# Attention preparation in small steps: 1/rms through ScalarE's ln and exp, and q and k scaled by ScalarE one token tile at a time

## The chip, the cores and the metric

The kernel runs on one core of a Trainium2 chip. The metric is device time in microseconds for one execution of the whole program (two layers of the trunk), median over runs. Five engines matter: TensorE (PE in the profile, with its weight loads as PEld), VectorE (DVE), ScalarE (ACT), GpSimd (POOL) and SyncE (SP), which issues the DMAs.

## The reference, cut to what matters

Two request groups share all weights: 128 context tokens ("prompt") and 1024 latent tokens. The change touches only the latent attention of each layer:

```
c_kv = _rmsnorm(kv_lat, kv_norm_g)
q = (_rmsnorm(q_lat, q_norm_g) @ w_q_up).reshape(b, t, MLA_HEADS, QK_HEAD)      # 8 heads of 96
q = _rmsnorm(q, q_head_g)
k, v = _mla_kv(c_kv, k_pe, w_kv_up, k_head_g)      # k = rmsnorm([k_nope 64, k_pe 32]) per head
if latent:
    q = jnp.concatenate([q[..., :64], _rope_2d(q[..., 64:])], axis=-1)
    k = jnp.concatenate([k[..., :64], _rope_2d(k[..., 64:])], axis=-1)
    k, v = concatenate with the cached context's k_c, v_c      # 1152 keys
attn = softmax(q k^T * 96 ** -0.5) v      # context tokens attend to themselves alone
```

So each token needs, per head, 1/rms of its 96 q elements and of its 96 k elements, a rotation of 32 of them, and a multiplication of all 96 by that 1/rms.

## The kernel before, in words

The eight heads are worked in four pairs. Everything is float32; a product that must be exact is split into a high and a low part and done as three matmuls.

`pair_prep` (L931) prepares a pair. For each of ten token tiles of 128 tokens (0 is the prompt, 1 to 8 the latent tokens, 9 the cached context) it issues nine matmuls (L960 to L969) into one PSUM tile, copies q, k and v out on ScalarE (L971 to L974) and collects sums of squares into `ssq` (L979, L981), then yields. After the ten tiles come a chain on VectorE: the sums are completed (L984 to L988), 1/rms is taken by `rsq` (L231: an integer guess and three Newton rounds, eleven instructions of 40 elements a partition), and for each half b of the tokens q is rotated (`rope`, L918 to L921), q is multiplied by 1/rms (L995, 768 elements a partition) and so is k (L997 for the 64 plain elements of each head, L998 for the rotated 32).

`prompt` (L1009) does the whole attention of the 128 context tokens of the pair: scaling (L1016 to L1019), transposes (L1022), scores (L1029), softmax (L1031 to L1039), and output (L1043 to L1050).

`head_prep` (L1057) transposes k and q of one head (L1070), splits them (L1073, L1074), then computes for 8 query tiles by 3 key chunks a score block (L1081) and its row maximum on VectorE (L1083), takes the maximum over all keys (L1087), negates it (L1088), transposes it (L1090) and writes it into the query operand (L1092).

`head_main` (L1098) is the attention of one head over nine key tiles. For each key tile: two halves of three score matmuls (L1127 to L1129) and an exp on ScalarE each (L1130) into PSUM tiles of which there are three; then, after a yield, the products with v (L1110) and, on GpSimd, the running sum of the exponentials (L1113, L1119, L1117). `head_end` (L1146) divides by that sum; it is issued in the next head's first key tile: L1153 on PE, L1157 and L1158 on ScalarE, L1159, L1160 and L1162 on VectorE.

The order of the work comes from `attention` (L1168). While `head_main` of head h runs, two side generators are advanced at each of its 18 or 19 yields: `heads()` (the next heads' `head_prep`, up to a weight RA per yield) and `pairs()` (the next pair's `pair_prep`, then GAP empty steps, then `prompt`, then the loads for the next stage), RB steps per yield. A pair's heads may start only when `R["ready", p]` is set. The framework then shifts neighbouring instructions a little. Each engine runs its own queue strictly in order, so one matmul that waits for VectorE holds everything behind it on PE.

Pair 0 and head 0 are prepared in the same way under the input projection (`in_proj`), in steps called from L783.

Of the kernel before, what the change touches and what calls it, by code (L numbers as in the profile page):

```python
# [25 lines left out]
P = 128  # L26
# [21 lines left out]


CT, CM, CB, RX = 0.7, 1.4, 0.7, 0.5  # L50
RA, RB, LEAD, GAP = 1.3, 0.7, 14, 5


def segs(c):
# [22 lines left out]
class Net:  # L77
# [653 lines left out]
    def in_proj(self, l, h, R, ticks):  # L731
        nc, a = self.nc, self.a
        rk, rv = R["rk"], R["rv"]
        rq, rg = [], []
        mix = R["mix"] = [None] * 8
        bg = []

        def step(n):
            for _ in range(n):
                while bg and next(bg[0], bg) is bg:  # L740
                    bg.pop(0)
        yc = {}
        for i in range(2, len(IN_FM)):
            name = IN_FM[i]
            kind, j = name[:2], int(name[2]) if name[2:] else int(name[1]) if name[1:].isdigit() else 0
            w = self.get(("in", l, i))
            if kind in ("rq", "rg", "gc"):
                dst = self.S(name)
            if kind == "q0":
                R["qn"] = [[self.S("qh", dt=F32R) for _ in range(2)], [self.S("ql", dt=F32R) for _ in range(2)]]  # L750
                sqq = self.S("sqq")
                qg = self.v("q_norm", l)
                pc = self.ax((P, 9, 1))
            if kind == "kv":
                R["ckv"] = [self.S("ch", dt=F32R), self.S("cl", dt=F32R)]
                kg = self.v("kv_norm", l)
                pc = self.ax((P, 9, 1))
                R["ckvo"] = self.sm("ckvo", (P, P), bufs=1)
            for c in range(3):
                cs = slice(c * CH, (c + 1) * CH)  # L760
                ps = self.mm()
                self.fm(w, h, KD, c, ps)
                if kind == "rg":
                    silu = nc.scalar.activation(dst[:, cs], ps, AF.Silu)
                elif kind == "xi":
                    self.conv_u(gc, u, ps, c)
                elif kind == "gb":
                    nc.vector.tensor_tensor(yc[j][:, cs], yc[j][:, cs], ps, op=ALU.mult)
                elif kind in ("q0", "q1"):
                    self.gain_split(ps, qg[:, j:j + 1], R["qn"][0][j][:, cs], R["qn"][1][j][:, cs])  # L770
                    if j == 0:
                        nc.scalar.activation(sqq[:, cs], ps, AF.Square)
                    else:
                        self.lat_sum(ps, pc, c == 0, c == 2, 3 * c, sqq[:, cs])
                elif kind == "kv":
                    self.gain_split(ps, kg, R["ckv"][0][:, cs], R["ckv"][1][:, cs])
                    self.lat_sum(ps, pc, c == 0, c == 2, 3 * c)
                    if c == 0:
                        nc.scalar.activation(R["ckvo"], ps[:, 0:P], AF.Copy, scale=kg)
                else:  # L780
                    nc.scalar.copy(dst[:, cs], ps)
                self.tick(ticks)
                step(3)  # L783
            if kind == "rq":
                rq.append(dst)
            elif kind == "gc":
                gc = dst
                u = gc
            elif kind == "xi":
                yc[j] = self.S("yc")  # L790
                self.conv_y(l, j, u, yc[j])
            elif kind == "gb":
                mix[j] = self.spill(yc[j])
            elif kind == "rg":
                rg.append(dst)
            elif kind == "q1":

                R["qms"] = self.sm("qms", (P, 9), bufs=1)
                nc.vector.tensor_scalar(R["qms"], pc.rearrange("p a b -> p (a b)"), EPS / 256, EPS * EPS, ALU.mult, ALU.add)
            elif kind == "kv":  # L800
                self.kv_scale(l, R, pc)
            if name == "rq1":
                bg.append(self.retention(l, rq, rk, rv, rg, mix))
            if name == "kv":
                step(1000)

                with self.tc.issue_after(silu.ins):
                    nc.scalar.preload_act_table_set("natural_log_exp_and_others")
            if name == "kv":
                self.mla_tables(l, R)  # L810
                self.pair_weights(l, 0, R)
                bg += [self.pair_prep(l, 0, R), self.head_prep(l, 0, R), self.prompt(l, 0, R)]
        step(1000)
# [98 lines left out]
    def rope(self, x, tab, out=None):  # L912
# [7 lines left out]
        nc.vector.tensor_tensor(out[:, :, :, 0:16], t1[:, :, :, 0:16], t2[:, :, :, 16:32], op=ALU.subtract)  # L920
        nc.vector.tensor_tensor(out[:, :, :, 16:32], t2[:, :, :, 0:16], t1[:, :, :, 16:32], op=ALU.add)  # L921

    def pair_weights(self, l, p, R):
        if ("w", p) not in R:
            raw = self.W()[:, :640]
            self.nc.sync.dma_start(out=raw, in_=self.a["w_qkv"][l, p])
            R["w", p] = self.S("qwh", (P, 640), F32R), self.S("qwl", (P, 640), F32R)
            self.hilo(raw, *R["w", p])
        return R["w", p]

    def pair_prep(self, l, p, R):  # L931
# [22 lines left out]
        for t in range(10):  # L954
# [25 lines left out]
            for j in range(2):  # L980
                nc.scalar.activation(sq[:, j, 0:64], kvp[:, j * 64:(j + 1) * 64], AF.Square, accum_out=ssq[:, 2 + j, t:t + 1])  # L981
            yield
        V = nc.vector
        V.tensor_tensor(ssq[:, 2:4, :], ssq[:, 2:4, :], R["kvs2"].unsqueeze(1).to_broadcast([P, 2, 10]), op=ALU.mult)  # L984
        V.tensor_tensor(ssq[:, 2:4, :], ssq[:, 2:4, :], R["kpss"].unsqueeze(1).to_broadcast([P, 2, 10]), op=ALU.add)
        V.tensor_scalar(ssq[:, 2:4, :], ssq[:, 2:4, :], 1.0 / 96, EPS, ALU.mult, ALU.add)
        V.scalar_tensor_tensor(ssq[:, 0:2, 0:9], ssq[:, 0:2, 0:9], 1.0 / 96,
                               R["qms"].unsqueeze(1).to_broadcast([P, 2, 9]), ALU.mult, ALU.add)  # L988
        r = self.rsq(ssq, (P, 4, 10))
        yield  # L990
        for b in range(2):
            self.rope(q[b][:, :, :, 64:96], R["rtab"][:, :, 4 * b:4 * b + 4])
            t0, n = 1 + 4 * b, 4 + b
            bc = lambda i, n, m: r[:, i:i + 2, t0:t0 + n].rearrange("p a b -> p b a").unsqueeze(3).to_broadcast([P, n, 2, m])
            V.tensor_tensor(q[b], q[b], bc(0, 4, 96), op=ALU.mult)  # L995
            yield
            V.tensor_tensor(k[b][:, :, :, 0:64], k[b][:, :, :, 0:64], bc(2, n, 64), op=ALU.mult)  # L997
            V.tensor_tensor(k[b][:, :, :, 64:96],  # L998
                            R["kper"][:, t0:t0 + n, :].unsqueeze(2).to_broadcast([P, n, 2, 32]), bc(2, n, 32), op=ALU.mult)
            yield  # L1000
        R["tm", p] = (lambda t: q[t // 4][:, t % 4], lambda t: k[min(t // 4, 1)][:, t - 4 * min(t // 4, 1)], vv)
        R["pr", p] = pr, prv, r
# [6 lines left out]
    def prompt(self, l, p, R):  # L1009
# [3 lines left out]
        at = self.attn_tile(p, R)  # L1013
        gains = self.gains(l)
        for hh in range(2):
            V.tensor_tensor(pr[:, hh, 64:96], pr[:, hh, 64:96], R["gq"], op=ALU.mult)  # L1016
            V.tensor_scalar(pr[:, hh, :], pr[:, hh, :], r[:, hh, 0:1], None, ALU.mult)
            V.tensor_scalar(pr[:, 2 + hh, 0:64], pr[:, 2 + hh, 0:64], r[:, 2 + hh, 0:1], None, ALU.mult)
            V.tensor_scalar(pr[:, 2 + hh, 64:96], R["kper"][:, 0, :], r[:, 2 + hh, 0:1], None, ALU.mult)  # L1019
        pt = self.ax((96, 4, P))  # L1020
        for i in range(4):
            nc.tensor.transpose(pt[:, i, :], pr[:, i, :], self.ident)  # L1022
# [6 lines left out]
            nc.tensor.matmul(ps[:, hh, :], qk[:, hh, :], qk[:, 2 + hh, :], start=True, stop=True)  # L1029
        m, den = self.sm("pm", (P, 2)), self.sm("pden", (P, 2))  # L1030
        V.reduce_max(m, ps, axis=AX.X)  # L1031
        V.tensor_scalar(m, m, -SCALE, None, ALU.mult)
        pp = self.Tt("pp", (P, 2, P))
        for hh in range(2):
            nc.scalar.activation(pp[:, hh, :], ps[:, hh, :], AF.Exp, scale=SCALE, bias=m[:, hh:hh + 1],
                                 accum_out=den[:, hh:hh + 1])
        V.reciprocal(den, den)
        for hh in range(2):
            V.tensor_scalar(pp[:, hh, :], pp[:, hh, :], den[:, hh:hh + 1], None, ALU.mult)  # L1039
        yield  # L1040
        pt = self.ax((P, 2, P))
        for hh in range(2):
# [14 lines left out]
    def head_prep(self, l, h, R):  # L1057
# [20 lines left out]
        for qt in range(8):  # L1078
            for c in range(3):
                ps = self.ax((P, CH))  # L1080
                nc.tensor.matmul(ps, qh[0:96, qt * P:(qt + 1) * P], kh[0:96, c * CH:(c + 1) * CH],  # L1081
                                 start=True, stop=True)
                nc.vector.reduce_max(mx[:, qt, c:c + 1], ps, axis=AX.X)  # L1083
                yield CM / 3
        yield CB
        mn = self.sm("mn", (P, 8))
        nc.vector.reduce_max(mn, mx, axis=AX.X)  # L1087
        nc.vector.tensor_scalar(mn, mn, -1.0, None, ALU.mult)  # L1088
        pt = self.ax((8, P))
        nc.tensor.transpose(pt, mn, self.ident)  # L1090
        o, _ = VEC["eye8"]
# [76 lines left out]
    def attention(self, l, R, x):  # L1168
# [10 lines left out]
        def pairs():  # L1179
            for p in range(1, 4):  # L1180
                yield from self.pair_prep(l, p, R)
                if p < 3:
                    self.pair_weights(l, p + 1, R)
                for _ in range(GAP):
                    yield
                R["ready", p] = True
                yield
                yield from self.prompt(l, p, R)
            while self.head_lim < 7:
                yield  # L1190
# [571 lines left out]
```

## Time and profile before

| | |
|---|---|
| median of 3 runs | 3169.8 us (3165.72 to 3171.39) |
| the profiled execution: its own time, its span | 3169.16 us, 3167.4 us |
| busy in the span: PE / DVE / ACT / POOL | 96% / 56% / 35% / 37% |
| attention of layer 0, of layer 1 (us of the span) | about 340 to 700, 1905 to 2260 |

A share of busy time is a mean over all stages; the two attention stretches are the ones this change touches, and they are read by themselves below. PEclk is the clock granted to TensorE as a share of 2.4 GHz: 0.50 is 1.2 GHz, and a value between the two is a mean over a window with both.

### The profile page before, as it was taken

The numbers are of one execution on the slowest core, as the hardware profiler recorded it, in microseconds if no ns is written. First come the engines' busy times: TensorE is split into PE (matmuls) and PEld (weight loads), VectorE is DVE, ScalarE is ACT, GpSimd is POOL, SyncE is SP. The second block draws the span as 40 slices with busy tenths as digits, with TensorE's granted clock in tenths as the row PEclk, the third lists the DMA queues.
The fourth block names the chain that finished last, engine by engine and source line by source line (L and its number), as shares of the span: only waits on it lengthen the run. The fifth ranks groups of instructions, "written<-read, shape, count | busy, mean of one in ns | idle before, by whom it ended". The sixth has DMA issues, their size and how long they took to land.

```text
span 3167.4 us, 48782 instructions
## 1 busy us (share of the span) xinstructions
PE 3033.0 (96%) x19136; PEld 2686.3 (85%) x19136; DVE 1778.7 (56%) x3483; ACT 1113.2 (35%) x2646; POOL 1178.4 (37%) x764
## 2 busy tenths in 40 slices
PE   6999999999799999999999999899988999999999
PEld 5988855459799999998999896554788999999999
DVE  6264476766954555633272646767588455556343
ACT  4333455444522222321153235454444222223211
POOL 3111243465643443411242103434656434343212
PEclk8999998999899999999999999999998999999999
DMA  5323000123222122576231110010322222226323
GB/s 211 103 95 128 22 12 1 60 91 107 83 81 74 63 84 81 178 251 237 66 113 48 49 32 13 12 53 8 121 100 69 84 84 71 69 71 220 101 67 100
DMA packets 126726, 278.06 MB, mean 88 GB/s; under 512 B 24097, under 2 KB 47393, under 8 KB 126497
## 3 DMA queue, kind: packets, MB, share of 16 engines
q1 hardware_dynamic: 126496, 274.95, 25.8%
q8 instruction: 151, 2.47, 0.3%
q14 instruction: 79, 0.64, 0.1%
HBM read 222.57 MB, written 52.33 MB: 87 GB/s over the span
## 4 chain that ended last, share of the span: by engine, by line
PE 81%; DVE 12%; DMA 2%; ACT 2%; issue 2%; POOL 1%; SPq 0%; DVEq 0%; POOLq 0%; ACTq 0%
PE mm L227 14%; PE mm L229 14%; PE mm L228 14%; PE ax L227 6%; PE ax L229 6%; PE ax L228 6%; PE ax L1110 5%; PE ax L1081 2%; PE mm L1127 2%; PE mm L1129 2%; PE mm L1128 1%; PE ax L325 1%; PE ax L1070 1%; DVE mx L1083 1%; POOL W L213 1%
## 5 line engine op out<-in xcount | busy, mean ns | idle before, releaser
L213 POOL TENSOR_TENSOR W<-r,W 128x512 fp32r<-128x512 f32 x336 | 447.8, 1346 | 541.7 <-ACT W L212 530.7
L213 POOL TENSOR_TENSOR W<-W,W 128x640 fp32r<-128x640 f32 (+5 forms) x168 | 298.4, 1777 | 827.9 <-ACT W L212 477.1
L227 PE MATMUL mm<-gh,W 128*128 128x384 f32 x1056 | 354.8, 336 | 1.9 <-DVE u L1401 1.1
L229 PE MATMUL mm<-gh,W 128*128 128x384 f32 x1056 | 353.3, 335 | 0.9 <-POOL W L213 0.8
L228 PE MATMUL mm<-gl,W 128*128 128x384 f32 x1056 | 352.9, 334 | 0.0
L1246 DVE SCALAR_TENSOR_TENSOR x<-mm,mod,x 128x128 f32<-128x128 f32 (+2 forms) x320 | 157.9, 515 | 329.7 <-PE mm L229 327.6
L229 PE MATMUL ax<-hth,W 128*128 128x288 f32 x1056 | 314.6, 298 | 10.1 <-POOL W L213 10.1
L227 PE MATMUL ax<-hth,W 128*128 128x288 f32 x1056 | 314.8, 298 | 7.6 <-ACT W L212 7.6
L228 PE MATMUL ax<-htl,W 128*128 128x288 f32 x1056 | 314.1, 298 | 0.0
L1119 POOL TENSOR_TENSOR W<-W,W 128x1024 f32<-128x1024 f32 x96 | 230.8, 2404 | 222.2 <-ACT W L1130 220.6
L212 ACT CAST W<-r 128x512 fp32r<-128x512 f32 x336 | 205.2, 621 | 184.8 <-DMA r<-in_w_up 63.8
L212 ACT CAST W<-W 128x640 fp32r<-128x640 f32 (+5 forms) x168 | 131.5, 783 | 390.6 <-DMA W<-in_w_down 178.7
L1083 DVE TENSOR_REDUCE mx<-ax 128x1 f32<-128x384 f32 x384 | 195.7, 550 | 115.2 <-PE ax L1081 112.8
L1130 ACT ACTIVATE W<-mm 128x512 f32<-128x512 f32 x288 | 168.5, 605 | 218.1 <-PE mm L1129 210.6
L227 PE MATMUL mm<-hh,W 128*128 128x384 f32 x704 | 240.5, 342 | 0.0
L229 PE MATMUL mm<-hh,W 128*128 128x384 f32 x704 | 239.0, 339 | 0.0
L228 PE MATMUL mm<-hl,W 128*128 128x384 f32 x704 | 237.9, 338 | 0.0
L1110 PE MATMUL ax<-W,vt 128*64 128x512 f32 x576 | 208.4, 658 | 8.2 <-DVE attn L1162 6.7
L229 PEld LDWEIGHTS ax<-hth,W 128*128 128x128 f32 x1056 | 201.2, 191 | 11.3 <-POOL W L213 11.3
L227 PEld LDWEIGHTS mm<-gh,W 128*128 128x128 f32 x1056 | 198.2, 188 | 13.0 <-issue 9.9
L227 PEld LDWEIGHTS ax<-hth,W 128*128 128x128 f32 x1056 | 201.4, 191 | 8.5 <-ACT W L212 8.5
L228 PEld LDWEIGHTS ax<-htl,W 128*128 128x128 f32 x1056 | 201.3, 191 | 0.0
(333 smaller groups left out, 7864.7 us busy)
## 6 DMA issues: line engine op xcount, KB each, us to landing
W<-in_ada_w SPq DMA_DIRECT2D x80, 512.0 KB, 5.1
gr<-gd SPq DMA_DIRECT2D x44, 576.0 KB, 5.4
r<-in_w_gate SPq DMA_DIRECT2D x96, 256.0 KB, 2.8
r<-in_w_up SPq DMA_DIRECT2D x96, 256.0 KB, 4.2
W<-in_w_in_fm SPq DMA_DIRECT2D x30, 512.0 KB, 3.7
W<-in_w_down SPq DMA_DIRECT2D x48, 320.0 KB, 3.5
gd<-gu SPq DMA_DIRECT2D x22, 576.0 KB, 3.7
gd<-gu SPq DMA_DIRECT2D x44, 224.0 KB, 2.2
```

What stands on the lines that cost most here:

```text
L212: self.nc.scalar.copy(hi, raw)
L213: self.nc.gpsimd.tensor_tensor(lo, raw, hi.bitcast(F32), op=ALU.subtract)
L227: self.nc.tensor.matmul(ps, wh, xh, start=first and i == 0, stop=False)
L228: self.nc.tensor.matmul(ps, wh, xl, start=False, stop=False)
L229: self.nc.tensor.matmul(ps, wl, xh, start=False, stop=last and i == n - 1)
L1081: nc.tensor.matmul(ps, qh[0:96, qt * P:(qt + 1) * P], kh[0:96, c * CH:(c + 1) * CH], start=True, stop=True)
L1083: nc.vector.reduce_max(mx[:, qt, c:c + 1], ps, axis=AX.X)
L1110: nc.tensor.matmul(po[64 * qc:64 * qc + 64, :], vv[:, kt, b:b + 64], prs[kt][:, qs], start=(kt == 0), stop=(kt == 8))
L1119: nc.gpsimd.tensor_tensor(acc, acc, prs[kt], op=ALU.add)
L1127: nc.tensor.matmul(ps, kh[0:104, ks], qh[0:104, qs], start=True, stop=False)
L1130: nc.scalar.activation(pr[:, qs], ps, AF.Exp, scale=SCALE)
L1246: self.nc.vector.scalar_tensor_tensor(x[m][:, t0:t1], ps[:, t0 - c * CH:t1 - c * CH], self.mod[l][:, j, m, i:i + 1], x[m][:, t0:t1], ALU.m ...
```

## The change

- `pair_prep`: the chain after the ten tiles is cut into more steps. 1/rms is started on ScalarE as exp(-0.5 ln x) and finished with one Newton round on VectorE (three instructions) in place of eleven. q and the plain part of k are multiplied on ScalarE, one token tile and head at a time (34 instructions a pair); the rotated part of k is multiplied on GpSimd.
- `prompt`: its scalings go to ScalarE, one product to GpSimd.
- `head_prep`: maximum and negation become one instruction.
- `attention`: RB goes from 0.7 to 1.0, the five empty steps to two; `in_proj` takes 4 steps where it took 3, once pair 0's preparation has begun.

By count: 45 more ScalarE instructions a pair, 27 fewer on VectorE, 4 more on GpSimd.

```diff
-RA, RB, LEAD, GAP = 1.3, 0.7, 14, 5
+RA, RB, LEAD = 1.3, 1.0, 14
...
-                step(3)
+                step(4 if i > 8 else 3)
...
+    def rope_steps(self, x, tab):
+        V = self.nc.vector
+        sh = [P, 4, x.shape[2], 32]
+        t1, t2 = self.Tt("rp1", sh), self.Tt("rp2", sh)
+        V.tensor_tensor(t1, x, tab[:, 0].unsqueeze(2).to_broadcast(sh), op=ALU.mult)
+        V.tensor_tensor(t2, x, tab[:, 1].unsqueeze(2).to_broadcast(sh), op=ALU.mult)
+        yield
+        V.tensor_tensor(x[:, :, :, 0:16], t1[:, :, :, 0:16], t2[:, :, :, 16:32], op=ALU.subtract)
+        V.tensor_tensor(x[:, :, :, 16:32], t2[:, :, :, 0:16], t1[:, :, :, 16:32], op=ALU.add)
+        yield
...
+        yield
         V.tensor_scalar(ssq[:, 2:4, :], ssq[:, 2:4, :], 1.0 / 96, EPS, ALU.mult, ALU.add)
...
-        r = self.rsq(ssq, (P, 4, 10))
+        r, t = self.sm("rsy", (P, 4, 10)), self.sm("rst", (P, 4, 10))
+        nc.scalar.activation(r, ssq, AF.Ln)
+        nc.scalar.activation(r, r, AF.Exp, scale=-0.5)
+        yield
+        V.tensor_tensor(t, r, r, op=ALU.mult)
+        V.scalar_tensor_tensor(t, t, -0.5, ssq, ALU.mult, ALU.mult)
+        yield
+        V.scalar_tensor_tensor(r, t, 1.5, r, ALU.add, ALU.mult)
         yield
         for b in range(2):
-            self.rope(q[b][:, :, :, 64:96], R["rtab"][:, :, 4 * b:4 * b + 4])
+            yield from self.rope_steps(q[b][:, :, :, 64:96], R["rtab"][:, :, 4 * b:4 * b + 4])
...
-            V.tensor_tensor(q[b], q[b], bc(0, 4, 96), op=ALU.mult)
-            yield
-            V.tensor_tensor(k[b][:, :, :, 0:64], k[b][:, :, :, 0:64], bc(2, n, 64), op=ALU.mult)
-            V.tensor_tensor(k[b][:, :, :, 64:96],
+            G.tensor_tensor(k[b][:, :, :, 64:96],
                             R["kper"][:, t0:t0 + n, :].unsqueeze(2).to_broadcast([P, n, 2, 32]), bc(2, n, 32), op=ALU.mult)
+            for t in range(n):
+                for j in range(2):
+                    if t < 4:
+                        nc.scalar.mul(q[b][:, t, j], q[b][:, t, j], r[:, j, t0 + t:t0 + t + 1])
+                    nc.scalar.mul(k[b][:, t, j, 0:64], k[b][:, t, j, 0:64], r[:, 2 + j, t0 + t:t0 + t + 1])
+                if t == 1:
+                    yield
             yield
...
-        nc.vector.reduce_max(mn, mx, axis=AX.X)
-        nc.vector.tensor_scalar(mn, mn, -1.0, None, ALU.mult)
+        nc.vector.tensor_reduce(mn, mx, axis=AX.X, op=ALU.max, negate=True)
...
-                for _ in range(GAP):
-                    yield
+                yield
+                yield
                 R["ready", p] = True
-                yield
                 yield from self.prompt(l, p, R)
```

In `prompt` the four scalings L1016 to L1019 become one GpSimd product and three ScalarE products, in two steps; L1032 and the two L1039 go to ScalarE.

The first place is VectorE's queue in layer 0 near the end of head 2's main loop, where the row maximum of head 3 is made: `mx` and `mn` are that maximum, `qt`, `kt` and `rsy` the pair 2's q, k and 1/rms. Before:

```order
L997 TENSOR_TENSOR kt_3991<-kt_3991,rsy_4409 128x8x64
L998 TENSOR_TENSOR kt_3991<-kper_2354,rsy_4409 128x8x32
L1083 TENSOR_REDUCE mx_4293<-ax_4489 128x1
L918 TENSOR_TENSOR rp_787_4492<-qt_3990,rtabq_2373 128x256
L919 TENSOR_TENSOR rp_788_4493<-qt_3990,rtabq_2373 128x256
L1087 TENSOR_REDUCE mn_4502<-mx_4293 128x8
L997 TENSOR_TENSOR kt_3992<-kt_3992,rsy_4409 128x10x64
L920 TENSOR_TENSOR qt_3990<-rp_787_4492,rp_788_4493 128x8x16
L921 TENSOR_TENSOR qt_3990<-rp_788_4493,rp_787_4492 128x8x16
L1088 TENSOR_SCALAR mn_4502<-mn_4502 128x8
L998 TENSOR_TENSOR kt_3992<-kper_2354,rsy_4409 128x10x32
```

Now:

```order
L928 TENSOR_TENSOR rp_782_4528<-qt_4025,rtabq_2373 128x256
L929 TENSOR_TENSOR rp_783_4529<-qt_4025,rtabq_2373 128x256
L1112 TENSOR_REDUCE mx_4385<-ax_4543 128x1
L1112 TENSOR_REDUCE mx_4385<-ax_4546 128x1
L931 TENSOR_TENSOR qt_4025<-rp_782_4528,rp_783_4529 128x8x16
L1115 TENSOR_REDUCE mn_4549<-mx_4385 128x8
L932 TENSOR_TENSOR qt_4025<-rp_783_4529,rp_782_4528 128x8x16
L1121 TENSOR_TENSOR W_4280<-ax_4556,vec_95 8x1024
```

The products with 1/rms have left this queue, and between the last `mx` and the finished `mn` stand one rotation step and one reduction where three vector instructions and two stages of `mn` stood.

The second place is ScalarE's queue in layer 0 at the end of head 0's main loop, where pair 1 is prepared and head 2's transposes come next on PE; L1159 is the exp of the scores, L1186 and L1187 belong to `head_end`. Before:

```order
L1130 ACTIVATE W_3788<-mm_3789 128x512
L1130 ACTIVATE W_3788<-mm_3794 128x512
L1157 ACTIVATE dy_3802<-ax_3799 128x512
L1158 ACTIVATE dy_3802<-dy_3802 128x512
L1130 ACTIVATE W_3816<-mm_3817 128x512
L212 CAST qwh_3812<-W_3810 128x640
```

Now, from the last two of twelve products in a run:

```order
L1021 ACTIVATE qt_3383<-qt_3383,rsy_3739 128x96
L1022 ACTIVATE kt_3385<-kt_3385,rsy_3739 128x64
L1159 ACTIVATE W_3815<-mm_3816 128x512
L1159 ACTIVATE W_3815<-mm_3821 128x512
L1186 ACTIVATE dy_3829<-ax_3826 128x512
L1021 ACTIVATE qt_3384<-qt_3384,rsy_3739 128x96
L1187 ACTIVATE dy_3829<-dy_3829 128x512
L1022 ACTIVATE kt_3386<-kt_3386,rsy_3739 128x64
L1021 ACTIVATE qt_3384<-qt_3384,rsy_3739 128x96
L1022 ACTIVATE kt_3386<-kt_3386,rsy_3739 128x64
```

All 34 products of the pair now stand in this queue, with four exps and the two instructions of `head_end` among them, ahead of head 2's copies.

## Rows read from the trace of the kernel before

**Rows 1.** The page: busy time by engine; the chain that ended last, by engine.
```profile
PE 3033.0 (96%) x19136; PEld 2686.3 (85%) x19136; DVE 1778.7 (56%) x3483; ACT 1113.2 (35%) x2646; POOL 1178.4 (37%) x764
...
PE 81%; DVE 12%; DMA 2%; ACT 2%; issue 2%; POOL 1%; SPq 0%; DVEq 0%; POOLq 0%; ACTq 0%
```

**Rows 2.** Windows: length, busy time (count) by engine, PEclk, DMA share, GB/s.
```profile
340.00:700.00 360.00, 336.12 (x1489) 199.36 (x1488) 249.51 (x440) 180.61 (x577) 164.36 (x81) 0.95 0.10 35
1905.00:2260.00 355.00, 331.44 (x1439) 194.09 (x1438) 245.16 (x432) 178.59 (x574) 161.96 (x77) 0.94 0.09 34
...
460.00:480.00 20.00, 18.09 (x68) 11.04 (x67) 16.99 (x40) 7.20 (x25) 8.95 (x4) 0.84 0.13 47
480.00:500.00 20.00, 16.30 (x61) 8.05 (x61) 16.84 (x23) 7.39 (x13) 9.97 (x7) 0.83 0.00 0
```

**Rows 3.** PE's waits, 390 to 730 us: total us, times, longest.
```profile
PE ax L1081 <- DVE mx L1083: 7.1, 4, 3.3
PE ax L1090 <- DVE kt L998: 3.7, 1, 3.7
PE ax L1110 <- DVE attn L1162: 3.4, 1, 3.4
PE ax L1070 <- DVE kt L998: 2.8, 1, 2.8
PE ax L1081 <- DVE W L1074: 1.4, 1, 1.4
PE ax L1022 <- DVE qt L1017: 1.2, 1, 1.2
PE ax L1081 <- DVE attn L1162: 0.9, 1, 0.9
```

**Rows 4.** PE's timeline at the wait of head 3's maximum: start, us, instruction, idle before.
```profile
475.96 0.44 PE L1081 MATMUL ax<-kTh,W 96*128 96x384 f32 x1 [1.77 <-DVE mx L1083]
491.88 0.38 PE L1090 MATMUL ax<-ident,mn 128*8 128x128 f32 x1 [3.69 <-DVE kt L998]
```

**Rows 5.** VectorE's timeline just before that wait ended.
```profile
488.41 2.42 DVE L921 TENSOR_TENSOR qt<-rp,rp 128x128 f32<-128x128 f32 x1
490.76 1.07 DVE L1088 TENSOR_SCALAR mn<-mn 128x8 f32<-128x8 f32 x1
```

**Rows 6.** GpSimd's timeline in the same stretch.
```profile
488.30 2.39 POOL L1119 TENSOR_TENSOR W<-W,W 128x1024 f32<-128x1024 f32 x1
```

**Rows 7.** VectorE's timeline earlier: the undisturbed twin of L921; pair 1's products.
```profile
399.63 0.28 DVE L921 TENSOR_TENSOR qt<-rp,rp 128x128 f32<-128x128 f32 x1
...
401.47 0.96 DVE L995 TENSOR_TENSOR qt<-qt,rsy 128x768 f32<-128x768 f32 x1
...
406.27 2.62 DVE L998 TENSOR_TENSOR kt<-kper,rsy 128x320 f32<-128x320 f32 x1
```

**Rows 8.** VectorE's groups of instructions, 390 to 730 us: count, busy us, mean ns.
```profile
L1088 DVE TENSOR_SCALAR mn<-mn 128x8 f32<-128x8 f32 x6 | 4.1, 676 | 0.1
...
L1087 DVE TENSOR_REDUCE mn<-mx 128x8 f32<-128x24 f32 x6 | 1.0, 174 | 0.1
```

**Rows 9.** Timeline: one score triple on PE; ScalarE products with a column, in a run.
```profile
390.73 0.40 PE L1127 MATMUL mm<-W,kTh 104*128 104x512 f32 x1
...
391.43 0.40 PE L1127 MATMUL mm<-W,kTh 104*128 104x512 f32 x1
...
139.54 0.97 ACT L508 ACTIVATE W<-W,lg 128x128 f32<-128x128 f32 x3
```

**Rows 10.** ScalarE's groups of instructions: the same products alone; the exp of the scores.
```profile
L508 ACT ACTIVATE W<-W,lg 128x128 f32<-128x128 f32 x16 | 5.4, 388 | 0.0
...
L1130 ACT ACTIVATE W<-mm 128x512 f32<-128x512 f32 x130 | 76.2, 603 | 103.3 <-PE mm L1129 98.4 <-POOL W L1119 2.8
```

**Rows 11.** The chain in order of time: the same four matmul instructions at either clock.
```profile
492.26 1.91 PE ax L1110 x4
...
532.25 1.01 PE ax L1110 x4
```

More of the change, by code (lines that the diff above doesn't have):

```diff
@@ L982, in pair_prep @@
             yield
-        V = nc.vector
+        V, G = nc.vector, nc.gpsimd
         V.tensor_tensor(ssq[:, 2:4, :], ssq[:, 2:4, :], R["kvs2"].unsqueeze(1).to_broadcast([P, 2, 10]), op=ALU.mult)
         V.tensor_tensor(ssq[:, 2:4, :], ssq[:, 2:4, :], R["kpss"].unsqueeze(1).to_broadcast([P, 2, 10]), op=ALU.add)
+        yield
         V.tensor_scalar(ssq[:, 2:4, :], ssq[:, 2:4, :], 1.0 / 96, EPS, ALU.mult, ALU.add)
@@ L1015, in prompt @@
         for hh in range(2):
[L1016 to L1019, printed above, removed]
+            nc.gpsimd.tensor_tensor(pr[:, hh, 64:96], pr[:, hh, 64:96], R["gq"], op=ALU.mult)
+            nc.scalar.mul(pr[:, 2 + hh, 0:64], pr[:, 2 + hh, 0:64], r[:, 2 + hh, 0:1])
+            nc.scalar.mul(pr[:, 2 + hh, 64:96], R["kper"][:, 0, :], r[:, 2 + hh, 0:1])
+        yield
+        for hh in range(2):
+            nc.scalar.mul(pr[:, hh, :], pr[:, hh, :], r[:, hh, 0:1])
+        yield
         pt = self.ax((96, 4, P))
@@ L1031, in prompt @@
         V.reduce_max(m, ps, axis=AX.X)
-        V.tensor_scalar(m, m, -SCALE, None, ALU.mult)
+        nc.scalar.mul(m, m, -SCALE)
         pp = self.Tt("pp", (P, 2, P))
@@ L1038, in prompt @@
         for hh in range(2):
-            V.tensor_scalar(pp[:, hh, :], pp[:, hh, :], den[:, hh:hh + 1], None, ALU.mult)
+            nc.scalar.mul(pp[:, hh, :], pp[:, hh, :], den[:, hh:hh + 1])
+        yield
         yield
@@ L1084, in head_prep @@
                 yield CM / 3
+        mn = self.sm("mn", (P, 8))
+        nc.vector.tensor_reduce(mn, mx, axis=AX.X, op=ALU.max, negate=True)
         yield CB
-        mn = self.sm("mn", (P, 8))
-        nc.vector.reduce_max(mn, mx, axis=AX.X)
-        nc.vector.tensor_scalar(mn, mn, -1.0, None, ALU.mult)
+        yield CB
         pt = self.ax((8, P))
@@ L1183, in pairs @@
                     self.pair_weights(l, p + 1, R)
-                for _ in range(GAP):
-                    yield
+                yield
+                yield
                 R["ready", p] = True
-                yield
                 yield from self.prompt(l, p, R)
```

## The prediction

> **What bounds the kernel now.** I read the busy times first, then the chain, then windows, then the waits of the stage that the change touches. TensorE is busy 96% of the span, and 81% of the chain that ended last is TensorE, 12% VectorE [rows 1]. So an edit off TensorE can only win back time in which TensorE stands idle or runs at the lower clock. Where is that? The two attention stretches [rows 2]: in layer 0 TensorE is busy 336.1 of 360 us, in layer 1 331.4 of 355, so it idles 23.9 + 23.6 = 47.5 us. The mean granted clock there is 0.95 and 0.94; since the two levels are 1.2 and 2.4 GHz, a mean of 0.95 means that a tenth of the stretch, 36 us, ran at 1.2 GHz (in layer 1 0.06 x 2 x 355 = 43 us). What that costs is seen on one kind of work: the same four products with v take 1.91 us at the lower clock and 1.01 at the upper [rows 11]. The ceiling of any change here is thus about 47 us of idle time and half of 79 us, some 85 us in all.
>
> The waits [rows 3] name VectorE for every large one. I sort those of layer 0 into places (layer 1 repeats them, its idle time is within 0.4 us):
> - P1, head 2's transposes behind pair 1's products, 2.8 + 1.2 = 4.0 us;
> - P2, behind `head_end` of head 1, 1.4 + 0.9 = 2.3 us;
> - P3, head 3's scores and maximum behind pair 2's chain, 1.77 + 3.69 = 5.5 us [rows 4];
> - P4, what the 7.1 us on L1083 leave without P3's 1.8 and one wait of 3.3 that lies in the loads for the next stage, 2.0 us, behind pair 2's `prompt` and a `head_end`;
> - P5, behind the `head_end` of head 3 and pair 3's Newton rounds, 3.4 us.
>
> Why is VectorE late when it is busy only 249.5 of 360 us [rows 2]? Look at P3. L921 takes 2.42 us [rows 5] where its twin takes 0.28 [rows 7], and it ends within 0.15 us of a GpSimd addition that had begun just before it [rows 5, 6]. Then the negation of eight numbers a partition, L1088, takes 1.07. Its mean over the stretch is 676 ns, while the reduction L1087, which has more to read, takes 174 [rows 8]. So small VectorE instructions on SBUF are held for the rest of a GpSimd addition of 2.4 us, and each instruction of this kind that stands in front of something TensorE needs is a lot that can be drawn. The change removes 27 of them a pair.
>
> **The change, part by part**, in terms per layer, three pairs each (pair 0 lies under the input projection, where its steps have other matmuls to hide behind; I cost it at nothing, and if 72 steps were too few, a remainder would run bare).
>
> VectorE's products and Newton rounds go. In P3's queue (first place of the order above) the products with 1/rms are gone, and between the last maximum and `mn` stand one rotation instruction and one reduction of the unheld kind. A rotation can still be held once (2.42 - 0.28 = 2.1 us), and TensorE covers part of that: of 5.5 us I take 5.0 as won, and keep 3 as the lower end. In P5 two of the instructions in front were Newton rounds; `head_end`'s own two stay. I take half, 1.7. In P2 and P4 `head_end` stays and only some neighbours go: half again, 2.3/2 + 2/2 = 2.2. Sum 8.9 us of idle time.
>
> ScalarE's added work. Before, nothing multiplies 96 or 64 elements by a column on ScalarE. The nearest rows are products of 128 elements from SBUF to SBUF: 388 ns alone [rows 10], but 0.97 us for three in a run [rows 9], which is (0.97 - 0.39)/2 = 0.29 from start to start. I take 0.27 in a run, since there are fewer elements, and keep 0.39 as the upper bound. A pair's 34 products are then 9.2 us, all 45 instructions 12 us. Three pairs bring 36 us to the 180.6 that ScalarE is busy in 360 [rows 2]: 60%, so on average it is covered. Locally it is not. At P1 (second place of the order) 34 products, four exps of 0.6 us [rows 10] and two instructions of about that length stand in a row: 9.2 + 2.4 + 1.2 = 12.8 us. In the trace VectorE did pair 1's products from 401.5 to 408.9, in 7.4 us [rows 7], and this already cost P1's 4.0 us. So the operands are 5.4 us later. Against that TensorE now has three more score halves ahead of the transposes, 0.70 us each (three matmuls, 390.73 to 391.43 [rows 9]), and some scores, together near 3 us, and the transposes can follow the products tile by tile. I take +2 us at P1. For pairs 2 and 3 the new order mixes products and exps, but an exp behind several products holds a PSUM tile of which there are three: +1.5 us for both.
>
> The Trainium skill speaks against this part: "ScalarE: Activation LUTs", section "Rules for kernel authors", says to put a multiplication on VectorE rather than on ScalarE, because VectorE is the faster of the two for it. The trace agrees on the engine's own time: 768 elements take VectorE 0.96 us in one instruction [rows 7], and ScalarE would need eight of them, 8 x 0.27 = 2.2 us. What the rule would make of the whole time is the first rival.
>
> The clock. Idle time and lower clock go together here: around P3 the clock is 0.84 and 0.83 in two windows of 20 us [rows 2]. A mean of 0.83 loses 0.17 x 20 = 3.4 us of full-speed work. If P3 goes I take the second window whole and half of the first (3.2/2 = 1.6): 5.0 us. P1's stays.
>
> The wider steps. RB 1.0 in place of 0.7 makes a pair ready earlier; 30 steps a pair now, 24 before. No head waits for `ready` alone in the rows, so I give this nothing, with up to 2 us either way by where the pieces fall. GpSimd's four more products a pair are small beside its additions (2.4 us each [rows 6]) and it is busy 164 of 360 us; but a product ahead of the last addition can delay the sum that `head_end` needs by 1 us, which is within P1's +2. Ln and Exp are already in use in the same stage, so no table load comes with them.
>
> Sum per layer: -8.9 + 2 + 1.5 - 5.0 = -10.4 us, for two layers -21. The profiled execution took 3169.2 us (span 3167.4); it is within 1 us of the median of the three runs, so the same number serves for both: 3169 - 21 = **3148 us**. By the bounds: with P3 at 3, P2, P4 and P5 unchanged, P1 at +4 and the clock giving back half, the sum is -3 + 4 + 1.5 - 2.5 = 0; with P2 to P5 gone (13.2), P1 no worse, no new waits and 10 us of clock, it is -23 a layer, 3123 us.
>
> **The rivals.**
> *ScalarE becomes the bound (slower).* Its place is the exp in `head_main`: behind a group of products it frees its PSUM tile too late, and TensorE waits for L1130. Price: if the products run at 0.39 apiece and not at 0.27, the 45 instructions of a pair take 5.4 us more, and where the queue is full all of it falls on TensorE; six pairs, 32 us, so 3148 + 32 = 3180 us. It decides from about 0.35 a product, where 21 us are used up. For it: ScalarE is full at P1. Against it: the run at 0.29 [rows 9]; and PE's waits for ScalarE are none of the large ones now [rows 3]. The rule named above would make the time come out on this side.
> *The waits only move (no change).* GpSimd's additions are as many as before, the chain of sums, rotations and `head_end` stays on VectorE, and the lot may fall on another instruction in front of TensorE; P3 would return as a wait of the next head. Then only 5 us are won and the clock stays: 3164 us. For it: P2 and P5 have `head_end` in front, which is untouched.
> *It wins more.* Fewer holds on VectorE and a TensorE that stays at the upper clock: P2 to P5 go with their clock, 3115 to 3123 us. Against it: the wait of 3.3 us in the loads and `head_end` have nothing to do with this change.
>
> **How the numbers follow.** Differences under 0.2%, 6.3 us, can't be told from no change here. Forecast 0.55, ScalarE as the bound 0.14, waits that move 0.18, more 0.13. The forecast's own cases lie from 3128 to 3163; the waits that move around 3164, so they are split, a third of them still faster by over 6.3 us, two thirds within it, and a little of ScalarE's rival is within it too. That gives faster 0.72, same 0.15, slower 0.13. For 8 in 10 I leave out the upper half of ScalarE's rival and the lower part of the larger gain: 3118 to 3173.
>
> **What would show it.** Right: PE's waits on L998 and L1017 at the pair's products are gone, and the wait before the transpose of the maximum is under 1 us; VectorE is busy less in each attention stretch (81 instructions fewer), ScalarE some 36 us more; the clock at head 2's end is 1.0; at P1 PE now waits for ScalarE's products (L1022 of the new text), 4 to 6 us. Wrong: products at 0.35 us or more from start to start; waits of PE for the exp that sum to over 10 us a layer; or an idle time of TensorE in the attention stretches that is still above 40 us in sum.

## The result and the profile after

The changed kernel took 3129.5 us (median of 4 runs, 3126.3 to 3132.0); the kernel before, on the same chip, 3169.7 (3165.7 to 3171.4). The ratio is 0.9877, with a 95% interval of 0.9862 to 0.9893: 40 us faster, where 21 were forecast. The profiled execution took 3131.7 us with a span of 3130.0.

The page of the changed kernel, busy time and the chain that ended last, by engine (against [rows 1]):

```profile
PE 3023.2 (97%) x19136; PEld 2683.0 (86%) x19136; DVE 1666.8 (53%) x3267; ACT 1197.4 (38%) x3006; POOL 1197.2 (38%) x796
...
PE 83%; DVE 9%; ACT 3%; issue 2%; DMA 1%; POOL 1%; SPq 0%; DVEq 0%; POOLq 0%; ACTq 0%
```

The span fell by 37.4 us. TensorE's busy time fell by 9.8 (3033.0 to 3023.2) with the same number of matmuls; the mean granted clock of the execution rose from 0.977 to 0.982. The rest, 27.6, is idle time of TensorE: 134.4 before (3167.4 - 3033.0), 106.8 now. Where was it? The windows of the same stretches, columns as in [rows 2]:

```profile
340.00:700.00 360.00, 350.16 (x1633) 216.50 (x1633) 210.48 (x363) 219.16 (x725) 180.88 (x99) 0.98 0.12 42
...
1890.00:2250.00 360.00, 350.17 (x1637) 216.68 (x1636) 208.46 (x361) 218.45 (x724) 183.07 (x96) 0.98 0.12 43
...
460.00:480.00 20.00, 20.00 (x69) 10.08 (x69) 16.89 (x32) 12.85 (x39) 12.39 (x9) 1.00 0.05 17
480.00:500.00 20.00, 18.91 (x100) 12.06 (x102) 13.29 (x23) 16.16 (x53) 10.29 (x8) 1.00 0.01 1
```

TensorE idles 9.8 us in each attention stretch, where it was 23.9 and 23.6: 27.8 us, all of the net gain in idle time. VectorE is busy 39 us less in the first stretch, ScalarE 38.5 more, 61% of it. The two windows around head 3's maximum, at 0.84 and 0.83 before, are at 1.00. So is the window at P1, the kernel before first:

```profile
400.00:420.00 20.00, 15.95 (x63) 8.85 (x63) 19.17 (x29) 9.41 (x17) 10.50 (x6) 0.83 0.00 1
```
```profile
400.00:420.00 20.00, 17.93 (x78) 9.64 (x79) 8.59 (x16) 17.53 (x53) 11.84 (x7) 1.00 0.00 1
```

TensorE's waits from 340 to 730 us, total, times and longest (against [rows 3]):

```profile
PE ax L1110 <- DVE mx L1112: 3.6, 1, 3.6
PE ax L1099 <- DVE kTl L1103: 1.7, 1, 1.7
PE ax L1182 <- POOL W L1146: 1.2, 2, 0.9
PE ax L1139 <- ACT W L1159: 0.9, 1, 0.9
PE ax L1099 <- ACT kt L1022: 0.9, 2, 0.5
PE ax L972 <- DVE attn L1191: 0.6, 1, 0.6
```

The first is the wait in the loads for the next stage, untouched (3.3 before). The other rows of this view sum to 6.1 us, two small ones not shown; before, without the loads' wait, it was 20.1. The 3.7 before the transpose of head 3's maximum [rows 4] is gone.

At P1, ScalarE now scales pair 1's q and k. Its timeline (start, us, instruction, idle before), and VectorE's when 1/rms was finished:

```profile
395.19 0.38 ACT L1021 ACTIVATE qt<-qt,rsy 128x96 f32<-128x96 f32 x1 [0.82 <-DVE rsy L1010]
395.48 0.33 ACT L1022 ACTIVATE kt<-kt,rsy 128x64 f32<-128x64 f32 x1
395.71 0.36 ACT L1021 ACTIVATE qt<-qt,rsy 128x96 f32<-128x96 f32 x1
395.98 0.57 ACT L1159 ACTIVATE W<-mm 128x512 f32<-128x512 f32 x1
...
397.17 0.36 ACT L1021 ACTIVATE qt<-qt,rsy 128x96 f32<-128x96 f32 x1
397.44 0.34 ACT L1022 ACTIVATE kt<-kt,rsy 128x64 f32<-128x64 f32 x1
397.68 0.37 ACT L1021 ACTIVATE qt<-qt,rsy 128x96 f32<-128x96 f32 x1
```
```profile
394.97 0.19 DVE L1010 SCALAR_TENSOR_TENSOR rsy<-rst,rsy 128x40 f32<-128x40 f32 x1
```

A product follows the one before by 0.23 to 0.29 us, 0.25 on average from 397.17 on. 1/rms is there at 395.2, where VectorE's first product began at 401.5 before [rows 7]: 6.3 us earlier.

At pair 3 ScalarE's products do delay TensorE. Seven of them in a row end with the first line; the copy of the next head's k stands behind them, VectorE waits for that copy and TensorE for VectorE, and after eight more products TensorE waits for an exp:
```profile
531.20 0.34 ACT L1022 ACTIVATE kt<-kt,rsy 128x64 f32<-128x64 f32 x1
531.44 1.24 ACT L1102 ACTIVATE kTh<-ax,vec 96x512 fp32r<-96x512 f32 x2
```
```profile
532.14 1.40 DVE L1103 SCALAR_TENSOR_TENSOR kTl<-ax,vec,kTh 96x512 fp32r<-96x512 f32 x2 [3.24 <-ACT kTh L1102]
```
```profile
532.94 0.64 PE L1099 MATMUL ax<-ident,qt 128*96 128x128 f32 x4 [1.72 <-DVE kTl L1103]
...
535.23 2.45 PE L1139 MATMUL ax<-W,vt 128*64 128x512 f32 x4 [0.95 <-ACT W L1159]
```

### The profile page after: what moved, and what is told of

It reads as the page before. It is cut to its first block, busy times and chain, and to the rows that moved or that the text cites. A ratio compares the mean times of both kernels' runs of the same rounds, so it can differ in the third digit from the quotient of the medians.

```text
span 3130.0 us, 48980 instructions
## 1 busy us (share of the span) xinstructions
PE 3023.2 (97%) x19136; PEld 2683.0 (86%) x19136; DVE 1666.8 (53%) x3267; ACT 1197.4 (38%) x3006; POOL 1197.2 (38%) x796
## 4 chain that ended last, share of the span: by engine, by line
PE 83%; DVE 9%; ACT 3%; issue 2%; DMA 1%; POOL 1%; SPq 0%; DVEq 0%; POOLq 0%; ACTq 0%
PE mm L227 14%; PE mm L229 14%; PE mm L228 14%; PE ax L227 6%; PE ax L228 6%; PE ax L229 6%; PE ax L1139 5%; PE ax L1110 3%; PE mm L1156 2%; PE mm L1157 2%; PE mm L1158 2%; PE ax L325 1%; PE ax L1099 1%; DVE hb L1392 1%; DVE hy L1414 1%
## 5 line engine op out<-in xcount | busy, mean ns | idle before, releaser
L1159 ACT ACTIVATE W<-mm 128x512 f32<-128x512 f32 x288 | 167.1, 603 | 148.4 <-PE mm L1158 140.9
L1139 PE MATMUL ax<-W,vt 128*64 128x512 f32 x576 | 205.7, 626 | 1.9 <-ACT W L1159 1.9
```

What stands on the lines that cost most here:

```text
L1139: nc.tensor.matmul(po[64 * qc:64 * qc + 64, :], vv[:, kt, b:b + 64], prs[kt][:, qs], start=(kt == 0), stop=(kt == 8))
L1159: nc.scalar.activation(pr[:, qs], ps, AF.Exp, scale=SCALE)
```

## Experiments

Three theories. **H**: the change takes small SBUF instructions off VectorE, which GpSimd's additions hold. **P**: the faster steps carry the gain. **S**: ScalarE has no room. In the diffs, `-` is the kernel named.

**1. Pacing alone, on the kernel before.**
```diff
-RA, RB, LEAD, GAP = 1.3, 0.7, 14, 5
+RA, RB, LEAD = 1.3, 1.0, 14
-                step(3)
+                step(4 if i > 8 else 3)
-                for _ in range(GAP):
-                    yield
-                R["ready", p] = True
+                yield
+                yield
+                R["ready", p] = True
-                yield
```


> The kernel before with the change's pacing alone: RB 1.0, two empty steps between a pair's products and its release in place of five and one behind it, and four steps a piece for the late pieces of the input projection; every instruction stays on its engine. Theory H (holds): before, small VectorE instructions on SBUF, up to 0.28 us long, are held up to 2.4 us behind GpSimd's additions and stand ahead of what TensorE needs; pacing moves none of them off VectorE, so 3155 to 3172 us (before 3169.8, the change 3129.5). Theory P (pacing): 1/rms comes 6.3 us earlier in the changed kernel because the steps are taken faster, and this carries the gain, so 3130 to 3145 us.

Measured 3190.9 us, ratio 1.0067 (1.0052 to 1.0082): slower by 20 us, which neither theory expected. TensorE's waits over the whole run:
```profile
PE ax L1022 <- DVE qt L1017: 35.3, 6, 7.7
```
In the kernel before this row is 2.4 us in 2 waits. With pairs 1 to 3 released earlier in both layers, TensorE comes to the prompt's transposes before VectorE has got that far. P, that the pacing carries the gain by itself, falls.

**2. The changed kernel with the old pacing** (the diff of 1 the other way round).

> The changed kernel with the pacing of the kernel before: RB 0.7, five empty steps and one, three steps a piece throughout; the work stays on ScalarE and GpSimd and in its smaller steps. H: most of the gain stays, 3130 to 3145 us. P: most of it goes, 3155 us or more. In between if a pair's chain, with more and smaller steps taken at 0.7 a step, comes later and the heads wait for it at line 1099.

3146.3 us (3135.0 to 3150.5), 0.9921 (0.9899 to 0.9943): 1 us above the range of H, far under what P gave; these four runs lie further apart than those of the other kernels. The work on other engines and in smaller steps brings some 24 us by itself; the same pacing that cost 20 on the old code brings 17 on the new.

**3. The products of q and k back on VectorE, in the changed kernel.**
```diff
-            G.tensor_tensor(k[b][:, :, :, 64:96],
-            for t in range(n):
-                for j in range(2):
...
+            V.tensor_tensor(q[b], q[b], bc(0, 4, 96), op=ALU.mult)
+            yield
+            V.tensor_tensor(k[b][:, :, :, 0:64], k[b][:, :, :, 0:64], bc(2, n, 64), op=ALU.mult)
+            V.tensor_tensor(k[b][:, :, :, 64:96],
...
```


> The changed kernel with the products of q and k back on VectorE as six whole instructions a pair (0.96 to 2.6 us each before); Ln and Exp, the prompt's scalings on ScalarE and the negated maximum stay. H: these six are long instructions, 9 to 11 us of VectorE's time a pair, and head maxima and evictions queue behind them, so a third to a half of the 40 us goes, 3142 to 3152 us. P: within 5 us of the changed kernel. A theory S (ScalarE has no room to spare) says it gets faster than 3129.5, as 34 products a pair leave ScalarE.

3125.9 us, 0.9863 (0.9846 to 0.9879): not to be told from the changed kernel. The part that gives the change its name adds nothing that shows. VectorE's timeline at P1 in this kernel:
```profile
393.56 0.19 DVE L1010 SCALAR_TENSOR_TENSOR rsy<-rst,rsy 128x40 f32<-128x40 f32 x1
...
394.00 3.13 DVE L1016 TENSOR_TENSOR qt<-qt,rsy 128x768 f32<-128x768 f32 x1
397.05 1.77 DVE L1018 TENSOR_TENSOR kt<-kt,rsy 128x512 f32<-128x512 f32 x1
...
401.69 0.48 DVE L1019 TENSOR_TENSOR kt<-kper,rsy 128x320 f32<-128x320 f32 x1
```
Even with 3.13 us for one product (0.94 for its twin) VectorE is through 8.2 us after it began; ScalarE's chain takes 12.4 (395.2 to 407.6). With 1/rms early, both are in time or nearly so. H named the wrong part here, and P's number for this run came true. S is not borne out: the waits for ScalarE's products go, but at pair 3 TensorE now waits 4.5 us in one piece for VectorE, where it waited 1.7.

**4. 1/rms by VectorE's eleven instructions again, in the changed kernel.**
```diff
-        nc.scalar.activation(r, ssq, AF.Ln)
-        nc.scalar.activation(r, r, AF.Exp, scale=-0.5)
...
+        r = self.rsq(ssq, (P, 4, 10))
```


> The changed kernel with 1/rms from the eleven VectorE instructions of the kernel before, with no empty steps taken out; all else as changed. H: eleven short instructions, each liable to a hold of 1 to 2.4 us, come back into the chain that ends in q and k: 1/rms comes 5 to 10 us later, and the pairs 2 and 3, two layers, lose 1 to 3 us each, so 3133 to 3142 us. P: within 4 us of the changed kernel. If the engine change of 1/rms is the main part, 3145 us or more.

3142.4 us, 0.9914 (0.9899 to 0.9929): 13 us of the gain hang on it, at the top of what H gave. VectorE's timeline, with 1/rms done at 401.2, 6 us later than in the changed kernel:
```profile
392.64 2.41 DVE L236 TENSOR_SCALAR rsy<-ssq 128x40 int32<-128x40 int32 x1
...
396.33 1.18 DVE L237 TENSOR_SCALAR rsy<-rsy 128x40 int32<-128x40 int32 x1
...
397.63 1.26 DVE L239 TENSOR_TENSOR rst<-rsy 128x40 f32<-128x40 f32 x1
...
401.02 0.20 DVE L241 SCALAR_TENSOR_TENSOR rsy<-rst,rsy 128x40 f32<-128x40 f32 x1
```
In the kernel before it was done at 401.4. TensorE's waits at P1 in this run are 3.1 us, where the changed kernel has 1.8; at pair 3 the wait of 1.7 has become 4.6:
```profile
401.95 1.07 PE L1176 MATMUL ax<-W,ones 128*64 128x512 f32 x2 [0.66 <-DVE W L1140]
...
405.93 0.50 PE L1150 MATMUL mm<-W,kTh 104*128 104x512 f32 x1 [2.01 <-ACT W L1153]
...
411.69 0.31 PE L1093 MATMUL ax<-ident,kt 128*96 128x128 f32 x1 [0.43 <-ACT kt L1016]
```

**5. The prompt's scalings back on VectorE, in the changed kernel** (lines 1041 to 1067).
```diff
-            nc.scalar.mul(pr[:, 2 + hh, 0:64], pr[:, 2 + hh, 0:64], r[:, 2 + hh, 0:1])
+            V.tensor_scalar(pr[:, 2 + hh, 0:64], pr[:, 2 + hh, 0:64], r[:, 2 + hh, 0:1], None, ALU.mult)
...
-        nc.scalar.mul(m, m, -SCALE)
+        V.tensor_scalar(m, m, -SCALE, None, ALU.mult)
...
```


> The changed kernel with the prompt's small scalings (of q, k and the rotated part, the negated maximum, the division by the denominator) back on VectorE, in the changed kernel's steps: 11 small SBUF instructions a pair, 176 ns on average unheld. After the first four runs (pacing alone 3190.9, products back on VectorE 3125.9) these and the negated head maximum are what is left to carry the gain. H: each is liable to a hold of up to 2.4 us, one in three to five is, and the heads' evictions queue behind, so +8 to +25 us on 3129.5. If they cost nothing, within 4 us, and the gain is the head maximum's or the steps'.

3145.9 us, 0.9927 (0.9913 to 0.9942): +16 us, as H had it. VectorE's timeline, and GpSimd's beside it:
```profile
482.74 1.53 DVE L1042 TENSOR_SCALAR qt<-qt,rsy 128x64 f32<-128x64 f32 x1
484.18 2.40 DVE L1043 TENSOR_SCALAR qt<-kper,rsy 128x32 f32<-128x32 f32 x1
486.50 1.21 DVE L1042 TENSOR_SCALAR qt<-qt,rsy 128x64 f32<-128x64 f32 x1
486.66 1.07 DVE L1043 TENSOR_SCALAR qt<-kper,rsy 128x32 f32<-128x32 f32 x1
```
```profile
482.62 1.59 POOL L213 TENSOR_TENSOR qwl<-W,qwh 128x640 fp32r<-128x640 f32 x1 [0.24 <-ACT qwh L212]
484.17 2.37 POOL L1148 TENSOR_TENSOR W<-W,W 128x1024 f32<-128x1024 f32 x1
486.60 1.05 POOL L1105 MEMSET kTh<- 8x1152 f32 x1
```
The three GpSimd instructions end at 484.21, 486.54 and 487.65; the held ones end at 484.27, 486.58, 487.71 and 487.73. Four scalings fill 5 us (482.74 to 487.73), and TensorE then waits 3.46 us at the transpose behind them.

**6. Maximum and negation apart, in the changed kernel; 7. the fused one alone, in the kernel before.** In 6 the reduction and the negation are two instructions at the changed kernel's place; in 7 the changed three lines replace the old ones.

> The changed kernel with the head maximum as a reduction and a negation apart, at the changed place (two empty steps of 0.7 ahead of the transpose). On the kernel before, the negated reduction alone gave nothing (3170.2). H: eight negations a layer in this stage, 609 ns on average with holds and up to 2.6 us, against 1.4 TensorE steps of slack ahead of the transpose: 3129 to 3136 us. If the fusion carries a part of the gain once the prompt's scalings are away, 3138 us or more.

> The kernel before with the head maximum as changed, alone: one reduction that negates, issued ahead of two empty steps of 0.7 instead of behind one, in place of a reduction and a negation straight ahead of the transpose that needs them. H: the waits of TensorE for the maximum (line 1090, 5.5 us at head 3, some at heads 1 and 2) go, 5 to 7 us a layer with what the clock gives back, so 3152 to 3162 us. If the gain needs all parts together, within 4 us of 3169.8.

In the changed kernel the separate negation costs 10 us (3139.4; 0.9902, 0.9884 to 0.9919), over the range that H gave, so the fusion does carry a part here: with a median of 946 ns and up to 2.4 us it is held more often than not. On the kernel before the fusion alone is worth nothing (3170.2; 1.0006, 0.9996 to 1.0015), against the 8 to 18 us that H gave: TensorE's wait at the transpose is 5.8 us there. The chain ahead of the maximum is as late as it was.

**8, 9. Without the sums.** Both kernels leave out the running sum of key tiles 0 to 7, that is, the additions that hold:
```diff
-                nc.gpsimd.tensor_tensor(acc, prs[0], prs[1], op=ALU.add)
+                nc.gpsimd.memset(acc, 1.0)
...
-            elif kt > 1:
-                nc.gpsimd.tensor_tensor(acc, acc, prs[kt], op=ALU.add)
```


> The kernel before without the running sum of key tiles 0 to 7 on GpSimd (seven additions of 2.4 us a head; a memset of ones stands for them, so the denominators hold key tile 8 alone): this part of the computation is left out. It takes away what holds VectorE's small instructions and nothing of VectorE's own work. H: the waits at heads 1 to 3 and at the release shrink in the kernel before by 6 to 10 us a layer in this stage and somewhat less in the rest, so 3130 to 3150 us. P, or that the chain of instructions is itself too long whatever holds it: within 8 us of 3169.8.

> The changed kernel without the same sum, the same part left out. H: the change has already taken most of what was held away, so at most 10 us below 3129.5, and the two kernels without sums stand within 15 us of each other. If they stay 30 us or more apart, the holds are not what the change removed.

3089.3 us for the kernel before (0.9757, 0.9741 to 0.9774), 3102.3 for the changed one (0.979, 0.9776 to 0.9805). Their pages, and the negation in the kernel before without sums over the whole run (610 ns on average with them):
```profile
PE 2998.0 (97%) x19136; PEld 2672.2 (87%) x19136; DVE 1676.8 (54%) x3483; ACT 1112.5 (36%) x2646; POOL 924.2 (30%) x668
...
L1088 DVE TENSOR_SCALAR mn<-mn 128x8 f32<-128x8 f32 x16 | 2.7, 170 | 0.4
```
```profile
PE 3006.5 (97%) x19136; PEld 2674.5 (86%) x19136; DVE 1617.3 (52%) x3267; ACT 1196.6 (39%) x3006; POOL 937.3 (30%) x700
```
The old instructions on the old engines, in the old order and pacing, are 80 us faster once these additions do not hold them. VectorE's busy time fell by 101.9 us (1778.7 [rows 1] to 1676.8) with the same 3483 instructions, which is how long the additions had held them. In the changed kernel the same edit takes 49.5 us from VectorE's busy time (1666.8 to 1617.3) and 27 us from the time. So the change saves 53 of the 80 us that the additions cost, and pays 13: without them it makes the kernel slower. H gave the old kernel 20 to 40 us, and it was twice as much; it gave the changed one at most 10, and it was 27. The 13 us between the two kernels are within the 15 that H gave.

**10, 11. The sums in four pieces**, on the kernel before and on that of experiment 3.
```diff
-                nc.gpsimd.tensor_tensor(acc, acc, prs[kt], op=ALU.add)
+                for s in range(0, 1024, 256):
+                    nc.gpsimd.tensor_tensor(acc[:, s:s + 256], acc[:, s:s + 256], prs[kt][:, s:s + 256], op=ALU.add)
```
(the first addition, of tiles 0 and 1, likewise)

> The kernel before with each GpSimd addition of the running sum in four pieces of 256 columns, same sums, nothing else. Without these additions the kernel before took 3089.3 us. H with a hold that ends with the GpSimd instruction: a held VectorE instruction waits for the end of a piece, some 0.6 us (a quarter of 2.4), not of a whole addition, so most of the 80 us comes back: 3100 to 3130 us, and the mean of the held groups falls towards that of the kernel without sums (the negation at line 1088 from 609 ns to under 350). Rival: the four pieces follow each other without a gap that VectorE could use, the hold lasts as long as before, and the pieces' own start-up is added: 3168 to 3185 us.

> A candidate for the fastest: the changed kernel with q and k scaled on VectorE in whole instructions again (3125.9 us in the third run) and the running sum in four pieces. H: 3098 to 3118 us (the changed kernel without sums took 3102.3). Rival as above: 3126 us or more.

On the kernel before, this one edit gives 3127.9 us (0.986, 0.9842 to 0.9878), inside the range of H and as much as the whole change. On top of experiment 3 it gives nothing: 3127.2 (0.9864, 0.9848 to 0.988), the rival's number; why the two gains do not add is open. The page of the kernel before with pieces, and two of its groups, GpSimd then VectorE:
```profile
PE 3021.6 (96%) x19136; PEld 2684.6 (86%) x19136; DVE 1769.6 (56%) x3483; ACT 1113.4 (36%) x2646; POOL 1244.7 (40%) x1100
...
L1121 POOL TENSOR_TENSOR W<-W,W 128x256 f32<-128x256 f32 x384 | 287.6, 782 | 131.6 <-ACT W L1132 131.4
...
L1088 DVE TENSOR_SCALAR mn<-mn 128x8 f32<-128x8 f32 x16 | 7.9, 496 | 0.4
```
Four pieces take 3.13 us where a whole addition took 2.40. In the first attention stretch the negation's longest fell from 2302 to 1494 ns, but its median rose from 172 to 366: holds are shorter and more of them. The mean did not come below the 350 ns that H wanted, and VectorE's busy time fell by 9.1 us only (1778.7 to 1769.6): it is held about as long in all. That the shorter single hold is what brings the 43 us back is argued, not shown.

**12. Pacing alone, without the sums.**

> The kernel before with the pacing alone (3190.9 us) and without the running sum of key tiles 0 to 7 on GpSimd, the same part left out as in the two runs without sums. Open is why the pacing by itself costs 21 us and gains 17 with the other parts: with it, TensorE comes to the prompt's transposes of pairs 1 to 3 before their products are ready (35.3 us in six waits on line 1017, 2.4 before). H: holds lengthen the chain ahead of line 1017, so without them the six waits fall under 10 us and the time is within 8 us of the kernel before without sums, 3089.3. Rival: the chain of VectorE instructions behind the last token tile is too long for the shorter gap by itself; the waits stay at 20 us or more and the time is 3105 us or more.

3141.5 us, 0.991 (0.9885 to 0.9934), 52 us over the kernel before without sums. TensorE's wait, and the page:
```profile
PE ax L1022 <- DVE qt L1017: 11.6, 8, 2.5
...
PE 3030.6 (96%) x19136; PEld 2688.2 (86%) x19136; DVE 1694.7 (54%) x3483; ACT 1113.1 (35%) x2646; POOL 934.0 (30%) x668
```
The time is the rival's; the waits lie between the two theories, as the additions made two thirds of the 35.3 us. Against the page of 8, TensorE is busy 32.6 us longer with the same matmuls and idles 21.4 longer (110.9 against 89.5). The old chain is too long for the short gap even without the additions.

## Why the prediction was right in direction and half in size

- **The clock: the sum right, its parts not.** Forecast were 5.0 a layer, all at P3; TensorE's busy time fell by 9.8 over the whole run. But P3's two windows gave back 6.6 us of full-speed work and not 5.0, P1's lower clock, which was to stay, went too (0.83 to 1.00 in 20 us, 3.4), and behind pair 3's new waits the clock is now 0.74 from 530 to 550 us. By the means of the two stretches (0.95 and 0.94, now 0.98) some 25 us came back, an estimate; why no more than 9.8 shows as busy time is open. So that 10 and 9.8 agree is in part luck.
- **The holds as the cause: right**, by experiments 5, 8 and 9: without the additions VectorE's same instructions are busy 102 us less in the kernel before and 50 less in the changed one. That the additions are what holds was read from one pair of rows [rows 5, 6]; the run without them brings the negation to 170 ns, level with the reduction.
- **The idle time at P1: the step that failed.** The forecast let 1/rms come at the same time as before, so that ScalarE's longer chain of 12.8 us cost +2. The chain took 12.4; but 1/rms came 6.3 us earlier, and what is left at P1 is 1.8 us, 0.9 for the products (4 to 6 were the sign to look for) and 0.9 for a sum of `head_end`, instead of 4.0: -2.2, a miss of 4.2 a layer. Two things make it earlier. With the Newton rounds back it is done at 401.2 (experiment 4), with the old pacing at 398.5 (experiment 2), with both parts at 395.2. I had costed Ln and Exp as two instructions on ScalarE and the pacing at nothing, and asked of neither when the chain would end. This is not the whole miss: in experiment 4, with 1/rms as late as before, P1 costs 3.1 us, so the early start is worth 1.3 of the 4.2. The other 2.9 are the size of the +2 itself: even from the old start, ScalarE's longer chain cost TensorE less than VectorE's. The 7.4 us that VectorE's was taken at held a product of 2.62 us [rows 7] whose like in experiment 3 took 0.48; how much of the 2.9 such holds are, no run shows.
- **P2 to P5 and pairs 2 and 3: the same sign, too small.** Forecast -8.9 and +1.5; these places held 13.2 us, short waits that I had not listed 2.9, and 4.3 is left of the 16.1: -11.8, a miss of 4.4 a layer. Of the 4.3, 2.7 are what +1.5 stood for, waits behind ScalarE's products: the 0.9 us of L1139 and the 1.7 of L1099 at pair 3. So that term was too small as well, and of the old waits 1.6 us are left. Over two layers, P1 and these miss 17 us, nearly the 19 between -21 and -40.
- **Which part earns it: wrong.** P3, the largest term, was credited to the fused maximum and the products' absence. Taken out of the changed kernel one at a time, the prompt's scalings cost 16 us, the old pacing 17 (give or take 7, by its interval), the Newton rounds 13, the separate negation 10, the products on VectorE -4, which is none that shows. These sum to more than 40, so they do not simply add: the pacing and the fused maximum, alone on the old kernel, give +20 and 0.
- **The wider steps: the bound of 2 us was wrong by about ten times**, in both directions. "No head waits for `ready` alone" was true, and beside the point: the steps also set how much VectorE must have done when TensorE arrives.
- **ScalarE as the bound: did not come.** 0.25 us a product, where 0.27 was taken and 0.35 was the point from which it decides; TensorE waits 0.9 us a layer for the exp, 2.7 with the copy behind the products. What the Trainium skill ("ScalarE: Activation LUTs", section "Rules for kernel authors") asks, multiplication on VectorE, came out neither faster nor slower (experiment 3, 3125.9 against 3129.5).
- **Two bounds without working.** The prediction doesn't say where 3115 in "it wins more" comes from (its parts give 3123), nor the 3128 to 3163 of the forecast's own cases.

Open: which part makes the changed kernel 13 us slower than the old one once the sums are gone, 3.0 of it idle time of TensorE (92.5 against 89.5) and 8.5 busy time by the two spans. No run took that apart. The runs without sums also let GpSimd give its buffers back sooner. That share was not measured by itself, but in the whole trace of the kernel before the waits of other engines for one of the additions left out are 2.8 us (ScalarE, once) and 4.5 (VectorE, twice), little beside 80. No version tried beats the changed kernel by more than can be told apart.

## What to carry to other kernels

When a short VectorE instruction on SBUF takes several times its usual duration, look at what GpSimd ran at that moment before moving work: shortening GpSimd's instructions, one edit here, gave as much as rewriting VectorE's side, though nothing on top of it. Cost a chain by when its last operand is ready, with everything that feeds it, not by its length alone. A knob that sets the pace is priced against the chain that it has to clear: the same one cost 20 us on the long chain and gave 17 on the short one.

## What the runs showed of the hardware that was not expected

- A GpSimd memset, which reads nothing, holds VectorE's scalings as an addition does: in experiment 5 two of them end at 487.71 and 487.73, with the memset of 1.05 us that ends at 487.65.
- The reduction of 24 numbers a partition, L1087, is not held in these traces: 179 ns at most in the kernel before over the whole run, 178 without the sums, where the negation behind it reached 2302 in the first attention stretch alone. The Trainium skill ("SBUF — State Buffer", section "Who interferes with whom") says that VectorE and GpSimd share a pair of SBUF ports, which one instruction locks to its end, that a `tensor_scalar` can need it whole and a reduction on this chip never does; these rows agree.
- An addition of 256 columns takes GpSimd 782 ns on average, a third of the 2404 for 1024 and not a quarter. A hold can outlast one piece: the negation's longest with pieces, 1494 ns, is nearly two.
- Idle time can cost more than itself: against experiment 8, experiment 12 has 21.4 us more of it and with it 32.6 us more of busy TensorE, at a mean granted clock of 0.980 in place of 0.989.
